# Half of the modulation columns as row sums on VectorE in a two-layer diffusion trunk

## The chip, the cores and the metric

The kernel runs on one core of a Trainium2 chip. The metric is the device time of one execution in microseconds (us); smaller is better. In the profile's names PE is TensorE (matmuls), PEld its weight loads, which overlap the matmuls, DVE is VectorE, ACT ScalarE, POOL GpSimd and SP SyncE, which issues most DMAs. L12 is line 12 of the kernel's source.

## What is computed

Two layers, each with the same weights for 256 latent tokens and 128 context tokens, 1024 wide. The conditioning vectors are `c` for the latent and `c_ctx` for the context tokens.

```
def _modulation(cvec, w_mod, b_mod):
    m = jax.nn.silu(cvec) @ w_mod + b_mod          # 1024 -> 6 x 1024
    return jnp.split(m[:, None, :], 6, axis=-1)

# each layer, for latent and context tokens with their own mod
h = _rms(x, g_mix) * (1.0 + mod[1]) + mod[0]
...                                                # input projection, three groups of attention heads (16 heads)
x = x + mod[2] * (concat(heads) @ w_out)
h = _rms(x, g_ffn) * (1.0 + mod[4]) + mod[3]
ffn = (silu(h @ w_gate) * (h @ w_up)) @ w_down     # 1024 -> 2816 -> 1024
x = x + mod[5] * ffn
```

So a layer has 6 x 1024 modulation values for each of two vectors. The kernel counts them in columns of 128: 0 to 15 are `mod[0]` and `mod[1]` (needed when a layer begins), 16 to 23 `mod[2]` (the attention's gate), 24 to 39 `mod[3]` and `mod[4]` (before the feed-forward), 40 to 47 `mod[5]` (the feed-forward's gate).

## The kernel before

All of it is float32. A big matmul is done as three: weights and activations are split into a high part of reduced precision and the rest, and `mm3` (L318 to L320) adds high x high, high x rest and rest x high. A block of weights arrives from memory in `raw` (three buffers, on SP's queue); ACT makes its high part `wh` (L251), DVE the rest `wl` (L257). The 384 tokens (256 + 128) lie along the free axis, so a matmul is 128x128 by 128x384. In `hh`/`hl`, `fh`/`fl`, `uh`/`ul` lie the two parts of a layer's normalised input, of the feed-forward's input and of its inner activations. PE's results go to PSUM banks named `z`, `s` and `t`.

A layer has four stages:

- *Attention* (layer 0 from the start to about 227 us, layer 1 about 541 to 731): input projection, 16 heads, and the first three of eight blocks of the output projection. Its order on every engine is written out by the kernel itself: a list planner with costs, priorities and earliest times sorts all pieces of work (`add(engine, cost, function, after=..., prio=..., ready=...)`), and the result is emitted as a manual schedule.
- *The rest of the out projection*, blocks m = 3 to 7. `gated` (L502) adds a gated result to the residual `xT`, `gain_split` makes `fh` and `fl`. From here on the framework's scheduler sets the order.
- *Feed-forward up* (L1521 onwards): 22 steps, each with a gate and an up group of 24 matmuls into one bank; then the tokens are scaled by `rb` (L1540), gated (L1545), and split into `uh` and `ul` (L1546, L1547).
- *Feed-forward down*: 8 groups of 66 matmuls and `gated` (L502). After layer 0's, a layer boundary in which a hand-written order on PE mixes the norm with modulation blocks.

The modulation is done by PE in sets of 16 columns (`ModSet`). A block is 128 rows of w_mod by 2048 columns, a load of 1 MB into `raw`; its four matmuls (L369) hold 32 columns of silu(cond) (`sv`) as weights, each in its own column group of the array, over 512 columns of w_mod; eight blocks make a set. Then ACT takes the sums out (`mev`, L375), PE turns them (L380, `t<-ident,mev`) and DVE adds the bias (L386) and writes `mods` (`mod` in the profile); `mod_aff` (L415) makes `aff` from (1 + scale) x gain. Where the sets run:

- layer 0, columns 0 to 15: at the very start, in four parts with their own weights; these blocks have 128 columns by four column groups (`m<-qu,sv`, `m<-ku,sv`).
- layer 0, columns 16 to 31 and 32 to 47: 16 blocks in layer 0's attention, in the planner's list (`blocks`, with earliest times by `SPREAD`).
- layer 1, columns 0 to 15: 8 blocks in layer 0's attention too (`EXTRA`).
- layer 1, columns 16 to 31: blocks 0 to 5 at the layer boundary (`BUB`), the rest in layer 1's attention. The first four come from `early` tiles, loaded by POOL's queue during layer 0's feed-forward, into the room of `hh`, `hl`, `fh` and `fl`.
- layer 1, columns 32 to 47: 8 blocks in layer 1's attention.

`parameters(l)` fetches a row of gains for a layer, spread over the partitions, into `prow` (L534), and DVE makes rotary tables and a lambda of it (L545, L551, L555, L561). For layer 1 it is called in the code between up and down part of layer 0's feed-forward, but waits for nothing there, and the scheduler put it into the end of layer 0's attention.

Of the kernel before, what the change touches and what calls it, by code (L numbers as in the profile page):

```python
# [39 lines left out]
SPREAD = ((15, 3), (60, 9))  # L40
DOWN = (0, 0, 0, 0, 0, 0, 0, 0)

# [136 lines left out]
@with_exitstack  # L179
def trunk(ctx: ExitStack, tc, xT_d, cv_d, pcol_d, prow_d, cache_d, dfk_d, rope_d, bias_d, ident_d,  # L180
          w_mod, w_mod0, w_in, w_uq, w_ukv, w_out, w_gate, w_up, w_down, yT_d, new_d):
    nc = tc.nc
# [151 lines left out]
    class ModSet:  # L334


        def __init__(self, l, q, pre=(), part=None):
            self.l, self.q, self.pre, self.w = l, q, pre, {}
            self.kb = 0
            if part is None:  # L340
                self.n, self.cols = 512, [2048 * q + 512 * g for g in range(4)]
            else:
                n = self.n = 512 // PARTS
                self.cols = [2 * n * part, 2 * n * part + n, 1024 + 2 * n * part, 1024 + 2 * n * part + n]
            self.part, self.step = part, 512 // self.n

        def load(self, kb, *kind):
            if self.part is not None and kind[0] != "raw":
                t = [v.rearrange("p h t -> p (h t)")[:, :1024] for v in self.room()]
            elif self.part is not None:  # L350
                t = raw.tile([P, 2, 1024], F32, tag="raw", name=nm("raw"))
                t = [t[:, i] for i in range(2)]
            if self.part is not None:
                for i in range(2):
                    nc.sync.dma_start(t[i], w_mod0[self.part, kb // self.step, :, i])
                self.w[kb] = [v.rearrange("p (k c) -> p k c", k=self.step) for v in t]
            elif kb < len(self.pre):
                self.w[kb] = self.pre[kb]
            elif self.part is None:
                self.w[kb] = load(mod_rows(self.l, kb, self.cols[0]), [2048])  # L360

        def mm(self, kb):
            if kb == 0:
                self.pm = bank(ps_m, "m")
            w, n = self.w.pop(kb), self.n
            for k in range(self.step):
                for g in range(4):
                    ws = w[:, g * n:(g + 1) * n] if self.part is None else w[g // 2][:, k, (g % 2) * n:(g % 2) * n + n]
                    nc.tensor.matmul(self.pm[32 * g:32 * g + 32, :n], sv[:, kb + k, :], ws,  # L369
                                     start=(kb + k == 0), stop=(kb + k == KD - 1), tile_position=(0, 32 * g))  # L370
            self.kb = kb + self.step
# [10 lines left out]
        def bias(self):  # L382
            nb = self.n // P
            for g in range(4):
                c0 = self.cols[g] // P
                nc.vector.tensor_tensor(  # L386
                    mods[self.l][:, c0:c0 + nb, :], self.pt[:, :nb, 32 * g:32 * g + 2],
                    pcol[self.l][:, PC_BMOD + c0:PC_BMOD + c0 + nb].unsqueeze(2).to_broadcast([P, nb, 2]), op=ALU.add)
            if self.part is not None:
                mod_aff(self.l, 0, KD // PARTS * self.part, KD // PARTS * (self.part + 1))  # L390
            elif self.q != 1:
                mod_aff(self.l, self.q // 2, 0, KD)

        def steps(self):
            for kb in range(self.kb, KD):
                self.load(kb)
                self.mm(kb)
                yield
# [130 lines left out]

    def parameters(l):  # L530

        pc = pcol[l]
        prow = par.tile([P, PR_W], F32, tag="prow", name=nm("prow"))
        fetch = lambda: (nc.sync if l == 0 else nc.gpsimd).dma_start(prow, prow_d[l:l + 1, :].to_broadcast([P, PR_W]))  # L534

# [36 lines left out]
    for l in range(DEPTH):  # L572
        pc = pcol[l]
        prow, naq, nlam, subg, tabs, fetch, stages = made_params
        if l == 0:
            hh = act.tile([P, KD, NT], F32R, tag="hh", name=nm("hh"))
            hl = act.tile([P, KD, NT], F32R, tag="hl", name=nm("hl"))
            early = []
            mod_sets = {key: ModSet(*key, pre=early if key == (1, 1) else ()) for key in ((0, 1), (0, 2), (1, 0), (1, 1), (1, 2))}

# [78 lines left out]
        if l == 0:  # L659
# [776 lines left out]

        blocks = [(ms, kb, SPREAD[l][0] + SPREAD[l][1] * kb) for ms in (mod_sets[l, 1], mod_sets[l, 2]) for kb in range(ms.kb, KD)]
        blocks = [(ms, kb, SPREAD[l][0] + SPREAD[l][1] * i) for i, (ms, kb, _) in enumerate(blocks)]
        if l + 1 < DEPTH:
            blocks += [(mod_sets[l + 1, 0], kb, EXTRA[1] + EXTRA[2] * kb) for kb in range(EXTRA[0])]  # L1440
        prev, fin = None, first_mod
        gates = None
        for i, (ms, kb, r) in enumerate(blocks):
# [44 lines left out]
        if l + 1 < DEPTH:  # L1488
            mod_q.extend(mod_sets[l + 1, q].steps() for q in range(2) if mod_sets[l + 1, q].kb < KD)
        for key, w in ahead:  # L1490
# [26 lines left out]
        ul = ff.tile([P, KF, NT], F32R, name=f"ul{l}")  # L1517
        waiting = []
        for m in range(KF):
            pos = []  # L1520
# [13 lines left out]
            for mm, pos in waiting:  # L1534
# [12 lines left out]
                nc.vector.tensor_tensor(ul[:, mm, :], u, uh[:, mm, :].bitcast(F32), op=ALU.subtract)  # L1547
            waiting = []
        if l + 1 < DEPTH:
            for i in range(4):  # L1550
                pool, tag = (act, "hh") if i == 0 else (act, "hl") if i == 1 else (ff, f"fh{l}") if i == 2 else (ff, f"fl{l}")
                early.append(pool.tile([P, 2048], F32, tag=tag, name=nm("early")))
# [139 lines left out]
```

## Time and profile before

| | us |
|---|---|
| median of three runs | 1043.28 (1042.18 to 1043.92) |
| the profiled execution | 1044.4 |
| its span (first to last instruction) | 1042.2 |
| around the span | 2.2 |
| TensorE busy | 1025.5 (98%) |
| VectorE busy | 630.9 (61%) |
| ScalarE busy | 509.0 (49%) |
| GpSimd busy | 149.9 (14%) |

Starts in the profile count from the span's start. Matmuls are pipelined, and a busy PE need not be at its peak; weight loads (PEld) show how densely matmuls follow each other. PEclk is the granted clock of TensorE as a share of full speed. A view of time windows gives for each window the busy time of PE, PEld, DVE, ACT and POOL with the number of instructions, then the granted clock, the DMA engines' busy share, and GB/s.

### The profile page before, as it was taken

To read this page: it belongs to the slowest core of one execution; us is meant where nothing else is said; L and a number is where in the kernel's file an instruction comes from. 1 tells how busy PE (TensorE), PEld (TensorE's weight loads), DVE (VectorE), ACT (ScalarE), POOL (GpSimd) and SP (SyncE) were. 2 spreads that over 40 slices of the span, in tenths; PEclk is the share of its full clock that TensorE was granted. 3 is DMA by queue.
4 is the path that set the end of the run, shared out by engine and by line. 5 is a ranking of instruction groups with operands and counts; after the bars stand their busy time and mean duration, and the time that the engine had idled before them with its cause. 6 is when DMAs were issued, how large, how long until landed. Compare 5 with 4: busy or idle time off the path is not lost.

```text
span 1042.2 us, 16578 instructions
## 1 busy us (share of the span) xinstructions
PE 1025.5 (98%) x6212; PEld 931.2 (89%) x6212; DVE 630.9 (61%) x1447; ACT 509.0 (49%) x1179; POOL 149.9 (14%) x221
## 2 busy tenths in 40 slices
PE   8999999999999999999999999999999999999998
PEld 7877777669999999999978977777999999999998
DVE  4677786767555555544446887777756555554332
ACT  3376777745433443333326567786644333343221
POOL 2266223200000000000016543240000000000000
PEclk9999999999999999999999999999999999999999
DMA  9865548745625343364444245552334344333541
GB/s 360 317 206 185 165 152 298 256 136 161 203 82 161 93 151 111 96 207 123 128 159 155 73 150 169 189 185 81 122 109 135 110 133 122 120 111 111 148 133 45
DMA packets 125999, 160.14 MB, mean 154 GB/s; under 512 B 4704, under 2 KB 111328, under 8 KB 120800
## 3 DMA queue, kind: packets, MB, share of 16 engines
q1 hardware_dynamic: 123552, 153.73, 45.9%
q0 software_dynamic: 784, 4.69, 1.2%
q8 instruction: 49, 0.80, 0.3%
q10 hardware_dynamic: 1584, 0.66, 0.2%
q14 instruction: 30, 0.25, 0.1%
HBM read 156.02 MB, written 3.05 MB: 153 GB/s over the span
## 4 chain that ended last, share of the span: by engine, by line
PE 88%; POOL 4%; DVE 4%; ACT 2%; issue 1%; DMA 1%; ACTq 0%; DVEq 0%; POOLq 0%
PE z L318 13%; PE z L320 12%; PE z L319 12%; PE t L319 6%; PE t L318 6%; PE t L320 6%; PE s L319 6%; PE s L318 6%; PE s L320 6%; PE m L369 4%; PE s L996 3%; POOL small L510 3%; PE t L963 2%; PE t L1098 2%; PE t L1335 1%
## 5 line engine op out<-in xcount | busy, mean ns | idle before, releaser
L251 ACT ACTIVATE wh<-raw 128x1024 fp32r<-128x1024 f32 (+2 forms) x216 | 201.6, 935 | 356.0 <-PE z L319 128.9
L257 DVE TENSOR_TENSOR wl<-raw,wh 128x1024 fp32r<-128x1024 f32 (+2 forms) x216 | 231.2, 1072 | 122.8 <-ACT wh L251 122.6
L318 PE MATMUL z<-fh,wh 128*128 128x386 f32 x304 | 103.2, 339 | 0.0
L319 PE MATMUL z<-fl,wh 128*128 128x386 f32 x304 | 103.0, 339 | 0.0
L320 PE MATMUL z<-fh,wl 128*128 128x386 f32 x304 | 102.6, 338 | 0.0
L318 PE MATMUL z<-wh,hh 128*128 128x384 f32 (+1 forms) x264 | 100.5, 381 | 0.9 <-ACT tok L1203 0.4
L320 PE MATMUL z<-wh,hl 128*128 128x384 f32 (+1 forms) x264 | 90.4, 342 | 0.5 <-DVE hl L490 0.3
L319 PE MATMUL z<-wl,hh 128*128 128x384 f32 (+1 forms) x264 | 89.7, 340 | 0.0
L510 POOL TENSOR_TENSOR small<-small,mhalf 128x4 f32<-128x4 f32 (+4 forms) x58 | 72.2, 1245 | 4.8
L318 PE MATMUL s<-fh,wh 128*128 128x386 f32 x200 | 68.2, 341 | 0.0
L318 PE MATMUL t<-fh,wh 128*128 128x386 f32 x200 | 68.1, 340 | 0.0
L319 PE MATMUL s<-fl,wh 128*128 128x386 f32 x200 | 67.8, 339 | 0.0
L319 PE MATMUL t<-fl,wh 128*128 128x386 f32 x200 | 67.7, 339 | 0.0
L320 PE MATMUL t<-fh,wl 128*128 128x386 f32 x200 | 67.5, 338 | 0.0
L320 PE MATMUL s<-fh,wl 128*128 128x386 f32 x200 | 67.5, 338 | 0.0
L1015 ACT ACTIVATE e<-s,small 128x384 f32<-128x384 f32 (+1 forms) x108 | 54.3, 509 | 16.3 <-DVE small L1004 15.2
L318 PEld LDWEIGHTS z<-wh,hh 128*128 128x128 f32 x264 | 49.8, 189 | 13.1 <-issue 8.2
L319 PEld LDWEIGHTS z<-fl,wh 128*128 128x128 f32 x304 | 57.5, 189 | 0.0
L320 PEld LDWEIGHTS z<-fh,wl 128*128 128x128 f32 x304 | 57.3, 188 | 0.0
L318 PEld LDWEIGHTS z<-fh,wh 128*128 128x128 f32 x304 | 57.2, 188 | 0.0
L996 PE MATMUL s<-ku,qu 96*128 96x384 f32 (+5 forms) x170 | 52.0, 411 | 0.6 <-ACT e L1015 0.6
L319 PE MATMUL z<-ul,wh 128*128 128x384 f32 x154 | 52.4, 340 | 0.0
(305 smaller groups left out, 2321.1 us busy)
## 6 DMA issues: line engine op xcount, KB each, us to landing
raw<-in_w_mod SPq DMA_DIRECT2D x36, 1024.0 KB, 5.1
raw<-in_w_gate SPq DMA_DIRECT2D x22, 1024.0 KB, 5.4
raw<-in_w_up SPq DMA_DIRECT2D x22, 1024.0 KB, 5.4
raw<-in_w_down SPq DMA_DIRECT2D x32, 704.0 KB, 4.5
raw<-in_w_in SPq DMA_DIRECT2D x40, 384.0 KB, 4.0
raw<-in_w_out SPq DMA_DIRECT2D x8, 1024.0 KB, 5.9
qu<-in_w_mod SPq DMA_DIRECT2D x8, 512.0 KB, 6.7
ku<-in_w_mod SPq DMA_DIRECT2D x8, 512.0 KB, 7.4
```

The source lines that it names most:

```text
L251: nc.scalar.activation(hi, src, AF.Copy)
L257: nc.vector.tensor_tensor(lo, src, hi.bitcast(F32), op=ALU.subtract)
L318: nc.tensor.matmul(out, sh, mh, start=first, stop=False)
L319: nc.tensor.matmul(out, sh, ml, start=False, stop=False)
L320: nc.tensor.matmul(out, sl, mh, start=False, stop=last)
L369: nc.tensor.matmul(self.pm[32 * g:32 * g + 32, :n], sv[:, kb + k, :], ws, start=(kb + k == 0), stop=(kb + k == KD - 1), tile_position=(0, ...
L510: nc.gpsimd.tensor_tensor(out, t[:, :n], mhalf[:, :n], op=ALU.pow)
L963: nc.tensor.transpose(pt[:, b, :], x, ident)
L996: nc.tensor.matmul(ps[:, i, :], q, k, start=True, stop=True)
L1015: nc.scalar.activation(x["e"][i], ps[:, j, :], AF.Exp, bias=x["mx"][:, i:i + 1], accum_out=x["su"][:, i:i + 1])
L1098: nc.tensor.matmul(po[64 * i:64 * i + 64, 0:NL], vv[:, b, v0 + i, :], p["pT"][i][:, b, :], start=(b == 0), stop=(b == 2), tile_position=(0 ...
L1335: nc.tensor.matmul(po, x["p"][:, b, :], vd[0][:, b if t < 2 else 3, h, :], start=(b == 0), stop=(b == nb - 1))
```

## The change

24 columns of the 48 of each layer, but in other places than before, are no longer computed by PE: a column is now 128 row sums of a product, one per partition. Its weights come transposed (`w_modT`, 128x1024, 512 KB) on POOL's queue into a ring of three slots in the room of `hl`; silu of the two vectors, broadcast over the partitions (`crow`, 1 MB), lies in the room of `hh`. For each column and each vector DVE runs one `tensor_tensor_reduce` over 128x1024, which starts from the bias and writes one column of `mods`; it is issued as two instructions, the main one and one that writes out the accumulator (both shown as `ISA` at L444). By layer:

- layer 0: PE keeps columns 16 to 31 (a set of 512-wide blocks, 8) and does 32 to 39 in 4 blocks of two row blocks and 256 columns; 40 to 47 are row sums in layer 0's feed-forward.
- layer 1: PE keeps 16 to 31; 0 to 15 and 32 to 39 are row sums in layer 0's feed-forward, 40 to 47 in layer 1's.

In layer 0's feed-forward that makes 32 columns (64 row sums), in layer 1's 8 (16). `ROWS_UP` and `ROWS_DOWN` say after which step of the loops the code issues how many columns; the scheduler places them. The loads of the `early` tiles move behind the last row sum. The parameter row of layer 1 lands in a tile in the room of `fl` (`staged`), which is free only after the last up matmul, and ACT copies it to `prow`.

```diff
@@ numbers
-DOWN = (0, 0, 0, 0, 0, 0, 0, 0)
+ROWSUMS = ((0, (40, 48)), (1, (0, 16)), (1, (32, 40))), ((1, (40, 48)),)
+ROWS_UP = (0, 0) + (1,) * 20
+ROWS_DOWN = (2, 3, 3, 4, 0, 0, 0, 0)
-EXTRA = (8, 135, 7)
@@ new class
+    class RowSums:
+        def __init__(self, parts):
+            self.todo = [(l, c) for l, (a, b) in parts for c in range(a, b)]
+            room = act.tile([P, 3 * DM], F32, tag="hh", name=nm("sums"))
+            self.s, self.junk = room[:, :2 * DM].rearrange("p (v k) -> p v k", v=2), room[:, 2 * DM:]
+            self.w = act.tile([P, 3, DM], F32, tag="hl", name=nm("wt"))
+            self.n = self.loaded = 0
+            nc.gpsimd.dma_start(self.s, crow_d.unsqueeze(0).to_broadcast([P, 2, DM]))
+            self.load()
+            nc.scalar.activation(self.s, self.s, AF.Silu)
+        def load(self):
+            while self.loaded < min(self.n + 3, len(self.todo)):
+                l, c = self.todo[self.loaded]
+                nc.gpsimd.dma_start(self.w[:, self.loaded % 3], w_modT[l, c * P:(c + 1) * P])
+                self.loaded += 1
+        def step(self, n):
+            for l, c in self.todo[self.n:self.n + n]:
+                for v in range(2):
+                    nc.vector.tensor_tensor_reduce(self.junk, self.w[:, self.n % 3], self.s[:, v], 1.0,
+                                                   pcol[l][:, PC_BMOD + c:PC_BMOD + c + 1], ALU.mult, ALU.add, mods[l][:, c, v:v + 1])
+                self.n += 1
+                self.load()
+                if l and c in (15, 39):
+                    mod_aff(l, c // 32, 0, KD)
@@ parameters
-        fetch = lambda: (nc.sync if l == 0 else nc.gpsimd).dma_start(prow, prow_d[l:l + 1, :].to_broadcast([P, PR_W]))
+        def fetch():
+            rows = prow_d[l:l + 1, :].to_broadcast([P, PR_W])
+            if staged is None:
+                nc.sync.dma_start(prow, rows)
+            else:
+                t = staged.tile([P, PR_W], F32, tag=f"fl{l - 1}", name=nm("staged"))
+                nc.gpsimd.dma_start(t, rows)
+                nc.scalar.activation(prow, t, AF.Copy)
@@ trunk: the sets
-            mod_sets = {key: ModSet(*key, pre=early if key == (1, 1) else ()) for key in ((0, 1), (0, 2), (1, 0), (1, 1), (1, 2))}
+            mod_sets = [[ModSet(0, 512, [2 * DM]), ModSet(0, 256, [4 * DM])], [ModSet(1, 512, [2 * DM], pre=early)]]
...
-        if l + 1 < DEPTH:
-            blocks += [(mod_sets[l + 1, 0], kb, EXTRA[1] + EXTRA[2] * kb) for kb in range(EXTRA[0])]
+        blocks = [(ms, kb) for ms in mod_sets[l] for kb in range(ms.kb, KD, ms.step)]
+        blocks = [(ms, kb, SPREAD[l][0] + SPREAD[l][1] * i) for i, (ms, kb) in enumerate(blocks)]
@@ feed-forward
+        sums = RowSums(ROWSUMS[l])
...
+            sums.step(ROWS_UP[m])
         if l + 1 < DEPTH:
-            for i in range(4):
-                ...
-                nc.gpsimd.dma_start(early[i], mod_rows(l + 1, i, 2048))
-            made_params = parameters(l + 1)
+            made_params = parameters(l + 1, ff)
...
-                if m < 7:
-                    mod_steps(DOWN[m])
+                sums.step(ROWS_DOWN[m])
+                if sums.n == len(sums.todo) and not early:
+                    for i, (pool, tag) in enumerate(((ff, f"fh{l}"), (ff, f"fl{l}"), (act, "hh"), (act, "hl"))):
+                        early.append(pool.tile([P, 2048], F32, tag=tag, name=nm("early")))
+                        nc.gpsimd.dma_start(early[i], mod_rows(l + 1, i, 2048))
```

`ModSet` now takes its columns as runs of a given width; a block of n columns by four groups covers 512 / n blocks of rows.

The first place is DVE in an up step of layer 0's feed-forward. `wl` is the rest of a weight block, `gt` the scaled and gated results, `ul` the rest of the inner activations. Before:

```order
L1538 COPY small_3796<-s_3740 128x2
L1540 TENSOR_TENSOR gt_3798<-s_3740,rb_3345 128x384
L257 TENSOR_TENSOR wl_3769<-raw_3765,wh_3767 128x1024
L1538 COPY small_3800<-t_3771 128x2
L1540 TENSOR_TENSOR gt_3802<-t_3771,rb_3345 128x384
L1545 SCALAR_TENSOR_TENSOR gt_3802<-gt_3802,small_3800,gt_3798 128x256
L1545 SCALAR_TENSOR_TENSOR gt_3802<-gt_3802,small_3800,gt_3798 128x128
L257 TENSOR_TENSOR wl_3812<-raw_3734,wh_3810 128x1024
L1547 TENSOR_TENSOR ul_3347<-gt_3802,uh_3346 128x384
```

And after (`sums` is the room with silu of the vectors, `wt` the ring of weights):

```order
L1578 COPY small_4278<-s_4224 128x2
L1580 TENSOR_TENSOR gt_4280<-s_4224,rb_3274 128x384
L444 ISA sums_3277,mod_102<-wt_3278,sums_3277,pcol_106 128x1024
L444 ISA mod_102 128x1
L260 TENSOR_TENSOR wl_4251<-raw_4172,wh_4249 128x1024
L1587 TENSOR_TENSOR ul_3276<-gt_4209,uh_3275 128x384
L444 ISA sums_3277,mod_102<-wt_3278,sums_3277,pcol_106 128x1024
L444 ISA mod_102 128x1
L1578 COPY small_4282<-t_4253 128x2
L1580 TENSOR_TENSOR gt_4284<-t_4253,rb_3274 128x384
L260 TENSOR_TENSOR wl_4299<-raw_4295,wh_4297 128x1024
```

Row sums stand ahead of each `wl`, two or three to a step. The second place is DVE at the end of layer 0's attention, from the last head's output `o` to the first `wl` that the out projection waits for. Before:

```order
L386 TENSOR_TENSOR mod_102<-t_3023,pcol_106 128x8 x4
L415 SCALAR_TENSOR_TENSOR aff_104<-mod_102,pcol_106 128x16
L1113 TENSOR_TENSOR o_2838<-t_3059,o_2837 128x384
L1512 TENSOR_TENSOR fl_3129<-mod_101,fh_3128 128x8x2
L502 SCALAR_TENSOR_TENSOR xT<-z_2825,mod_101,xT 128x256
L502 SCALAR_TENSOR_TENSOR xT<-z_2825,mod_101,xT 128x128
L502 SCALAR_TENSOR_TENSOR xT<-z_3003,mod_101,xT 128x256
L502 SCALAR_TENSOR_TENSOR xT<-z_3003,mod_101,xT 128x128
L257 TENSOR_TENSOR wl_3106<-raw_2681,wh_3089 128x1024
```

After:

```order
L1154 TENSOR_TENSOR o_2589<-t_3001,o_2588 128x384
L1551 TENSOR_TENSOR fl_3058<-mod_101,fh_3057 128x8x2
L534 SCALAR_TENSOR_TENSOR xT<-z_2741,mod_101,xT 128x256
L534 SCALAR_TENSOR_TENSOR xT<-z_2741,mod_101,xT 128x128
L534 SCALAR_TENSOR_TENSOR xT<-z_2791,mod_101,xT 128x256
L534 SCALAR_TENSOR_TENSOR xT<-z_2791,mod_101,xT 128x128
L534 SCALAR_TENSOR_TENSOR xT<-z_2986,mod_101,xT 128x256
L534 SCALAR_TENSOR_TENSOR xT<-z_2986,mod_101,xT 128x128
L529 SCALAR_TENSOR_TENSOR fl_3058<-xT,aff_103,fh_3057 128x256
L529 SCALAR_TENSOR_TENSOR fl_3058<-xT,aff_103,fh_3057 128x128
L529 SCALAR_TENSOR_TENSOR fl_3058<-xT,aff_103,fh_3057 128x256
L464 TENSOR_TENSOR sq_3039<-sq_3039,sq_3043 128x384
```

Directly behind it stands the `wl` of the out projection's block m = 3: three gates and four rows of the norm are now ahead of it, where two gates were. On PE the same place reads as follows after the change (`oxh` and `oxl` are the two parts of the head outputs that are ready early, `z_3071` is block m = 3):

```order
L321 MATMUL z_2986<-o_2588,wh_2637 128x384
L322 MATMUL z_2986<-o_2589,wh_2637 128x384
L323 MATMUL z_2986<-o_2588,wl_2839 128x384
L321 MATMUL z_3071<-oxh_133,wh_3030 128x384
L322 MATMUL z_3071<-oxl_134,wh_3030 128x384
L321 MATMUL s_3115<-oxh_133,wh_3074 128x384
L322 MATMUL s_3115<-oxl_134,wh_3074 128x384
L321 MATMUL z_3155<-oxh_133,wh_3078 128x384
L322 MATMUL z_3155<-oxl_134,wh_3078 128x384
L323 MATMUL z_3071<-oxh_133,wl_3048 128x384
```

Six matmuls that use only `wh` are ahead of the first that uses `wl_3048`. The third place is DVE where the down part begins; `prow`, `tab` and `lp` are layer 1's parameters, which stood in layer 0's attention before, and `raw_5066` is the weight block of the second down group:

```order
L586 TENSOR_SCALAR prow_4988<-prow_4988 128x32
L592 TENSOR_TENSOR tab_4993<-rope,prow_4988 128x2x32
L596 TENSOR_TENSOR tab_4993<-rope,prow_4988 128x2x2x8 x2
...
L602 TENSOR_TENSOR lp_5016<-prow_4988 128x64
L444 ISA sums_3277,mod_102<-wt_3278,sums_3277,pcol_106 128x1024
L444 ISA mod_102 128x1
L592 TENSOR_TENSOR tab_4995<-rope,prow_4988 128x2x32
L596 TENSOR_TENSOR tab_4995<-rope,prow_4988 128x2x2x8 x2
L260 TENSOR_TENSOR wl_5070<-raw_5066,wh_5068 128x768
```

The tables wait for the parameter rows, and the `wl` of the down part stands behind them.

More of the change, by code (lines that the diff above doesn't have):

```diff
@@ L334, in trunk @@
     class ModSet:
-        def __init__(self, l, q, pre=(), part=None):
-            self.l, self.q, self.pre, self.w = l, q, pre, {}
-            self.kb = 0
-            if part is None:
-                self.n, self.cols = 512, [2048 * q + 512 * g for g in range(4)]
-            else:
[L343 to L360, printed above, removed]
@@ new lines, in __init__, with load @@
+        def __init__(self, l, n, runs, part=None, pre=()):
+            self.l, self.n, self.part, self.pre, self.w = l, n, part, pre, {}
+            self.runs, self.per = runs, 4 // len(runs)
+            self.cols = [c + n * i for c in runs for i in range(self.per)]
+            self.step = 512 // n
+            self.kb = 0
+        def load(self, kb, *kind):
+            if kb < len(self.pre):
+                self.w[kb] = [self.pre[kb].rearrange("p (k c) -> p k c", k=1)]
+                return
+            nr, width = len(self.runs), self.n * self.per
+            if kind and kind[0] == "un":
+                t = [v.rearrange("p h t -> p (h t)")[:, :1024].rearrange("p (k c) -> p k c", k=self.step) for v in self.room()]
+            else:
+                t = raw.tile([P, nr, self.step, width], F32, tag="raw", name=nm("raw"))
+                t = [t[:, i] for i in range(nr)]
+            for i, c in enumerate(self.runs):
+                src = w_mod[self.l, kb * P:(kb + self.step) * P, c:c + width].rearrange("(k p) c -> p k c", p=P)
+                if self.part is not None:
+                    src = w_mod0[self.part, kb // self.step, :, i].rearrange("p (k c) -> p k c", k=self.step)
+                nc.sync.dma_start(t[i], src)
+            self.w[kb] = t
@@ L367, in mm @@
                 for g in range(4):
-                    ws = w[:, g * n:(g + 1) * n] if self.part is None else w[g // 2][:, k, (g % 2) * n:(g % 2) * n + n]
-                    nc.tensor.matmul(self.pm[32 * g:32 * g + 32, :n], sv[:, kb + k, :], ws,
+                    i = g % self.per
+                    nc.tensor.matmul(self.pm[32 * g:32 * g + 32, :n], sv[:, kb + k, :], w[g // self.per][:, k, i * n:(i + 1) * n],
                                      start=(kb + k == 0), stop=(kb + k == KD - 1), tile_position=(0, 32 * g))
@@ L390, in bias @@
                 mod_aff(self.l, 0, KD // PARTS * self.part, KD // PARTS * (self.part + 1))
-            elif self.q != 1:
-                mod_aff(self.l, self.q // 2, 0, KD)
+            elif self.cols[0] == 4 * DM:
+                mod_aff(self.l, 1, 0, KD)
         def steps(self):
-            for kb in range(self.kb, KD):
+            for kb in range(self.kb, KD, self.step):
                 self.load(kb)
@@ L1488, in trunk @@
         if l + 1 < DEPTH:
-            mod_q.extend(mod_sets[l + 1, q].steps() for q in range(2) if mod_sets[l + 1, q].kb < KD)
+            mod_q.extend(ms.steps() for ms in mod_sets[l + 1])
         for key, w in ahead:
@@ L1670 @@
     arrays, args = {}, []
-    order = ("xT", "cv", "pcol", "prow", "cache", "dfk", "rope", "bias", "ident", "w_mod", "w_mod0", "w_in", "w_uq", "w_ukv", "w_out", "w_gate", "w_up", "w_down")
+    order = ("xT", "cv", "crow", "pcol", "prow", "cache", "dfk", "rope", "bias", "ident", "w_mod", "w_mod0", "w_modT", "w_in", "w_uq", "w_ukv", "w_out", "w_gate", "w_up", "w_down")
     for n, v in ((n, feeds[n]) for n in order):
```

18 lines of the change are left out of this document (8 added, 10 removed).

## The prediction, made before the changed kernel was run

> **What bounds the kernel now.** I read the page first: the busy shares, the strips and the shares of the chain that ended last.
>
> ```profile
> span 1042.2 us, 16578 instructions
> PE 1025.5 (98%) x6212; PEld 931.2 (89%) x6212; DVE 630.9 (61%) x1447; ACT 509.0 (49%) x1179; POOL 149.9 (14%) x221
> ...
> PE   8999999999999999999999999999999999999998
> PEld 7877777669999999999978977777999999999998
> ...
> PEclk9999999999999999999999999999999999999999
> ...
> PE 88%; POOL 4%; DVE 4%; ACT 2%; issue 1%; DMA 1%; ACTq 0%; DVEq 0%; POOLq 0%
> ```
>
> TensorE works 98% of the span and carries 88% of the chain, so work taken from it should shorten the run. But the weight loads (PEld) fall to 6 to 8 tenths in two stretches, the two attention stages, and are full elsewhere. The next view gives each engine's busy time in stretches: layer 0's attention (four rows), the out projection's end, a feed-forward, and layer 1's attention (three rows).
>
> ```profile
> 100.00:150.00 50.00, 49.09 (x306) 35.88 (x305) 40.11 (x108) 36.93 (x124) 15.62 (x27) 1.00 0.56 182
> 150.00:200.00 50.00, 50.00 (x352) 36.10 (x350) 33.90 (x92) 34.25 (x113) 9.99 (x20) 1.00 0.78 268
> 200.00:225.00 25.00, 22.88 (x133) 14.75 (x130) 20.56 (x73) 15.83 (x46) 5.98 (x9) 0.93 0.54 173
> 225.00:265.00 40.00, 40.00 (x239) 39.11 (x237) 25.13 (x50) 20.46 (x38) 1.11 (x2) 1.00 0.48 163
> 300.00:350.00 50.00, 50.00 (x285) 50.00 (x284) 28.96 (x54) 20.03 (x30) 0.00 (x0) 1.00 0.40 125
> 600.00:650.00 50.00, 47.26 (x294) 36.70 (x295) 39.67 (x105) 35.98 (x115) 18.91 (x25) 1.00 0.49 161
> 650.00:700.00 50.00, 50.00 (x327) 39.36 (x327) 38.03 (x97) 39.62 (x130) 17.96 (x32) 1.00 0.57 189
> 700.00:730.00 30.00, 28.66 (x181) 20.48 (x175) 22.39 (x70) 19.30 (x62) 2.82 (x5) 0.94 0.26 86
> ```
>
> The first three numbers of a row after the length are PE, PEld and DVE. In the feed-forward (300 to 350) loads run 50.00 of 50: a saturated TensorE. From 150 to 200 PE also reads 50.00, but PEld 36.10, that is 0.72. There part of PE's "busy" is head work that a dependence stretches, and the dense matmuls and modulation blocks fill holes between the heads. DVE is at 0.68 to 0.80 there and at 0.58 in the feed-forward.
>
> The Trainium skill (Perfetto Trace Analysis, Identifying the Most-Contended Engine) says that matmul busy time is no good measure of how full TensorE is and that the busy share of weight loads is. By busy time the removed work would be worth all of itself, by the loads about seven tenths; the rows above agree with the page so far as the two do part in attention and not in the feed-forward.
>
> **1. Modulation blocks leave TensorE.** A block is four matmuls of 512 columns (8 records). Its tile's rows, two blocks in the chain, and a set's turn:
>
> ```profile
> L369 PE MATMUL m<-raw,sv x288: 592/593/1062, 52.6 to 707.3; 128*32 128x512 f32 x144
> L369 PE MATMUL m<-early,sv x32: 592/592/617, 537.4 to 542.6; 128*32 128x512 f32 x32
> ...
> 189.29 1.00 PE m L369 x8
> ...
> 220.36 1.87 PE m L369 x8
> ...
> 223.97 0.60 PE L380 MATMUL t<-ident,mev 128*128 128x128 f32 x4
> ```
>
> That is 320 records, 40 blocks, at 1.00 us each (the row at 189.29; the one at 220.36 ran at a low clock). In layer 0's attention stood 24 of them: the two sets of columns 16 to 47, and layer 1's first set. Now 8 blocks of 512 columns and 4 of two rows of 256 columns, as long by their elements, stand there: 12 fewer, 12.0 us. Layer 1 has 8 where it had 16: 8.0 us. A set also ends in a turn of 0.60: one and a half fewer in layer 0 (a half set has half a turn), one in layer 1. In all 12.9 + 8.6 = 21.5 us. The evacuations on ACT and the bias sums on DVE behind them go too; both engines have slack there, so they count nothing.
>
> What of it reaches the end lies between 0 (the heads' chains bind and holes merely stay empty) and 1. By the loads, 0.72 to 0.79 of TensorE's time in the main windows is real feed, and 0.59 (14.75 of 25) in layer 0's tail, 200 to 225, where heads run without enough filler. After the change that tail has 105 rows behind the last input-projection matmul on PE in place of 62 (135 for 107 in layer 1), so I take 0.65, between the two: **-14.0 us**; ends 0 and -21.5.
>
> **2. Layer 1's parameter rows leave layer 0's attention tail.** These stood there:
>
> ```profile
> 209.18 0.65 POOL L534 DMA_DIRECT2D prow<-in_prow  x1 [0.30 <-POOL brief L1162]
> 209.18 5.93 DMA prow<-in_prow
> 215.21 0.18 DVE L545 TENSOR_SCALAR prow<-prow 128x32 f32<-128x32 f32 x1 [1.03 <-DMA prow<-in_prow]
> 217.88 0.52 PE L963 MATMUL t<-ident,e 128*128 128x128 f32 x3 [2.11 <-DVE small L1020]
> ```
>
> DVE waited 1.03 us for the landing and then put the tables in front of a head's softmax; TensorE stood still 2.11 us, and the granted clock of that window was 0.93, 1.75 us of 25. Now nothing of it is there. At most 2.11 + 1.75 = 3.9 us come back; at least nothing, if the head is late anyway. I take **-3.0**: the wait goes surely, part of the clock's dip may stay in a tail with less filler.
>
> **3. The handover to layer 0's out projection.** In the new DVE order three pairs of gates, three modulated rows and a sum of squares stand before the first weight remainder (wl); before it was two pairs of gates. The rows that price them, and, for the next part, those of the feed-forward (300 to 400):
>
> ```profile
> L502 DVE SCALAR_TENSOR_TENSOR xT<-z,mod,xT 128x256 f32<-128x256 f32 x3 | 1.5, 484 | 3.6 <-PE z L320 3.6
> L502 DVE SCALAR_TENSOR_TENSOR xT<-z,mod,xT 128x128 f32<-128x128 f32 x3 | 1.0, 342 | 0.0
> ...
> L257 DVE TENSOR_TENSOR wl<-raw,wh 128x1024 fp32r<-128x1024 f32 x24 | 29.3, 1222 | 4.1 <-ACT wh L251 4.1
> L1547 DVE TENSOR_TENSOR ul<-gt,uh 128x384 fp32r<-128x384 f32 x12 | 6.6, 551 | 0.0
> L1545 DVE SCALAR_TENSOR_TENSOR gt<-gt,small,gt 128x256 f32<-128x256 f32 x12 | 5.8, 484 | 1.3
> L1540 DVE TENSOR_TENSOR gt<-z,rb 128x384 f32<-128x384 f32 x10 | 5.5, 549 | 0.0
> L1545 DVE SCALAR_TENSOR_TENSOR gt<-gt,small,gt 128x128 f32<-128x128 f32 x12 | 4.1, 346 | 0.0
> ...
> 197.99 1.22 DVE L257 TENSOR_TENSOR wl<-raw,wh 128x1024 fp32r<-128x1024 f32 x1
> 199.12 0.41 DVE L1179 TENSOR_REDUCE small<-brief 128x4 f32<-128x256 f32 x1
> ...
> 255.85 0.34 PE L318 MATMUL z<-fh,wh 128*128 128x386 f32 x1
> 443.73 0.34 PE L319 MATMUL s<-fl,wh 128*128 128x386 f32 x1
> 443.91 0.34 PE L320 MATMUL s<-fh,wl 128*128 128x386 f32 x1
> 444.08 0.34 PE L318 MATMUL z<-uh,wh 128*128 128x384 f32 x1
> ```
>
> On a full DVE the next instruction starts 0.09 us before the last one's end (197.99 to 199.12 is 1.13, not 1.22). So a pair costs 0.40 + 0.25, three pairs 1.95, the rows at the same shapes 1.05, the squares 0.46 (as 0.551 for 128x384), the remainder 1.13: 4.6 us from the first finished sum. TensorE has 12 matmuls to do meanwhile (the last six use wh alone), at 0.18 each (443.73 to 443.91) 2.1 us, and then waits: **+2.5**, between 0 (the sums finish earlier than I think) and 4.6. Before, 225 to 265 shows no idle time.
>
> **4. Row sums on VectorE.** No row of before has this instruction. Each column has two, each over 128x1024 with two fp32 inputs, and each is followed by an accumulator read. The nearest rows are L257, the same size with two inputs, and ACT's accumulator read:
>
> ```profile
> 198.69 0.21 ACT L1015 ACTIVATION_READ_ACCUMULATOR e<-s,small 128x1 f32 x1
> 198.78 0.59 ACT L1015 ACTIVATE e<-s,small 128x384 f32<-128x384 f32 x1
> ```
>
> Low end 1.13 + 0.09 = 1.22 us, high end 1.22 + 0.21 = 1.43; I take 1.3, as the reads follow closely. The order puts 59 of the 64 row sums of layer 0's feed-forward between the second up step and the second down step, some 21.5 up steps of 8.56 us ((444.08 - 255.85) / 22; the up part's first matmul is at 255.85): 184 us. DVE is free for 21.04 of 50 us there, so 77 us, 1.31 a row sum; taking the 0.09 off each of some nine instructions a step (two remainders, one rest of the product, six for the gating) frees 17 us more and makes it 1.6. 59 x 1.3 = 77 us fits, but nearly fills an in-order queue in which the wl of TensorE's next group stands behind one or two row sums. I count **+1.0**; ends 0 and (1.43 - 1.31) x 59 = +7. In layer 1's feed-forward 16 take 21 us of as much room: nothing.
>
> The Trainium skill (Vector Engine (DVE) Microarchitecture Reference, Points that are easy to get wrong) warns that the scalar-tensor-tensor shape with two sources in SBUF that are not bf16 runs at half rate, for want of a port for the accumulator. Against it stand the L1545 rows, which have such sources: 484 - 346 = 138 ns for 128 more elements, 1.08 ns each, as L257 has; but they don't use the accumulator, so the trace doesn't decide. At half rate a row sum would cost about 2.36; what that makes is the second rival.
>
> The weights of the sums (32 x 512 KB in 184 us, 91 GB/s beside 125, DMA share 0.40) come on POOL's queue, which has three slots, each due two columns (about 11 us) later, against 5.93 us for the landing above. ACT's one Silu of 128x2048 falls where ACT is free for 30 of 50 us. Both: nothing. The early loads of layer 1's blocks now start in the down part, behind the last sums, and have 50 us or more until 537: nothing.
>
> **5. The rows land after the last up matmul.** The landing slot is free at 444.08. With 5.93 us, an ACT copy behind one or two splits, and some dozen DVE instructions of 0.2 us, DVE reaches the next remainder about 10.4 to 11.8 us later; TensorE asks for it after one down group, 66 matmuls of 0.176, 11.6 us. **+0.5**, ends 0 and +3 if the landing is slow.
>
> **Sum.** -14.0 - 3.0 + 2.5 + 1.0 + 0.5 = -13.0. The profiled execution took 1044.4 us (span 1042.2 and 2.2 around it): 1031.4. It stands 1.1 above the median of 1043.28, so 1030.3: I say 1030.
>
> **Rivals.** *Everything taken off counts*, and the handover is hidden: -21.5 - 3.9 and nothing against it, 1018. For it: PE 50.00 of 50. Against: PEld 36.10.
> *Row sums too dear.* If one costs 2.36 us, 59 of them lack (2.36 - 1.45) x 59 = 54 us of room (1.45 is the middle of 1.31 and 1.6); DVE then sets the pace of layer 0's up part: 1084, slower. It decides from 1.45 + 13/59 = 1.67 us on; at 1.5 to 1.67 the run is between 1033 and 1043. The extrapolated slope of two-input rows speaks against it.
> *Heads bind.* The blocks filled holes that stay empty: only the rows' wait comes back, less the three losses: -3.0 + 4.0 = +1, about 1044; with a third of the credit (-7) 1037. For it: the tail's 0.59 and DVE's 40.11 of 50. Against: the tail without enough filler is 25 us long, the stretch in which blocks were spread over 100.
>
> **Chances.** Forecast (1020 to 1037) 0.57; full credit 0.12; heads bind 0.17, most of it between 1037 and 1043, some within a two-thousandth of before; row sums too dear 0.14, a fifth of that still faster. 0.2% is 2.1 us, about what a measurement of this kernel can tell from no change. Faster 0.83, same 0.05, slower 0.12. The range, 1016 to 1042, leaves out the dear row sums and the ends.
>
> **What would show it.** Right: L444's main row about 1.15 to 1.25 us, its read about 0.1 to 0.2; 300 to 350 with PE and PEld 50 of 50 and DVE above 0.9; layer 0's attention 8 us shorter or so, layer 1's 5; no prow row before the down part; one PE wait of 2 to 3 us at layer 0's out projection, released by a DVE wl. Wrong: PEld below 0.97 in layer 0's up part with PE waiting for wl (row sums), or the first out-projection matmul of a layer at the old time with lower PE share in the attention (heads).

## The result, and the profile after

The changed kernel takes 1036.14 us (median of four, 1035.75 to 1036.68) against 1042.73 us for the kernel before on the same chip (1041.92 to 1043.92): a ratio of 0.9935, 95% interval 0.9920 to 0.9949, so 6.6 us or 0.65% faster. The prediction said 1030, range 1016 to 1042. The time is in the range and the direction is right, but the gain is half of the 13 us forecast. The experiments show that the blocks moved out of layer 0's attention brought about what was forecast and that those moved out of layer 1's cost time. With two further losses, some 2 us are left of it beside the 4.2 us that the parameter rows bring alone.

The page of the changed kernel: span, busy shares, the strips of 40 slices, and the chain.

```profile
span 1034.4 us, 16528 instructions
PE 1012.3 (98%) x6074; PEld 933.0 (90%) x6074; DVE 719.5 (70%) x1599; ACT 509.1 (49%) x1180; POOL 172.7 (17%) x263
...
PE   8999999989999999999999999989999999999998
PEld 7877779679999999999978878867999999999998
...
PEclk9999999989999999999999999969999999999999
...
PE 76%; DVE 2%; ACT 1%; POOL 1%; issue 1%; ACTq 0%; DVEq 0%; POOLq 0%
L444 DVE CUSTOM_DVE_ANT_0 sums<-wt,sums,pcol 128x1024 f32<-128x1024 f32 x80 | 102.2, 1278 | 0.3 <-DVE small L1578 0.3
```

DVE has 89 us more work, as planned, and PE 13 us less. The 80 row sums are 40 columns of the 96 of both layers, 8 of layer 0 and 32 of layer 1, not 24 of each layer. The line to look at is PEclk: before it was 9 in every slice, now there is an 8 and a 6. Over the whole span the granted clock fell:

```profile
core 0: 1042.2 us, clock 0.995
```

```profile
core 0: 1034.4 us, clock 0.986
```

The first row is before, the second after. Before lost 0.005 x 1042.2 = 5 us of TensorE's clock, after 14.5 us, although after does less on TensorE. Where this happens shows in windows of the changed kernel (columns: PE, PEld, DVE, ACT, POOL busy, granted clock, DMA share, GB/s). First the end of layer 0's attention, then layer 1's attention tail, then layer 0's up part, and the start of the down part:

```profile
220.90:227.73 6.83, 4.41 (x14) 4.41 (x15) 5.98 (x10) 2.04 (x6) 0.00 (x0) 0.50 0.47 147
674.88:678.29 3.41, 2.29 (x15) 1.68 (x14) 2.53 (x7) 2.99 (x12) 2.95 (x5) 1.00 0.77 261
678.29:698.77 20.48, 18.98 (x61) 11.92 (x63) 13.61 (x41) 12.15 (x43) 5.82 (x11) 0.50 0.05 14
698.77:702.18 3.41, 3.41 (x27) 2.98 (x24) 2.55 (x7) 2.44 (x7) 0.44 (x1) 1.00 0.21 58
245.00:433.00 188.00, 188.00 (x1071) 187.73 (x1070) 170.88 (x316) 75.37 (x115) 17.99 (x33) 1.00 0.64 210
433.00:480.00 47.00, 47.00 (x270) 45.92 (x269) 28.63 (x61) 16.64 (x23) 3.18 (x6) 1.00 0.75 234
```

From 678.29 to 698.77 TensorE ran at exactly half clock, for six times 3.41 us, and PE reads 18.98 of 20.48. The chain that ended last stays on PE from 678.62 to 699.66 but for some 1.2 us, so PE is the bound there, at half speed. The layer's last input-projection matmul starts at 673.99; what follows is heads alone, where before the modulation blocks stood between them. The window ahead of the drop has PE busy for 2.29 of 3.41 us only.

The stages, each from its first matmul to the next stage's, in us; the last column is (1 - granted clock) x span, to about 0.5 us, since the clock has three digits.

| | layer 0: attention and out projection | up | down and boundary | layer 1: attention and out projection | clock lost |
|---|---|---|---|---|---|
| before | 233.5 | 188.2 | 100.9 | 212.5 | 5.2 |
| after | 224.4 | 188.3 | 102.2 | 213.5 | 14.5 |
| rows only (e3) | 229.6 | 188.3 | 100.9 | 210.9 | 1.0 |
| rows early (e4) | 230.1 | 188.3 | 102.3 | 213.6 | 17.7 |
| earlier wl (e2) | 220.3 | 188.3 | 102.2 | 213.5 | 10.3 |
| spare matmuls (e1) | 224.7 | 188.2 | 102.2 | 209.2 | 3.1 |
| L1 blocks back (e5) | 225.0 | 188.2 | 100.9 | 211.1 | 3.1 |

Layer 0's attention gained 9.1 us, layer 1's, with 8 blocks fewer, lost 1.0, and the down part lost 1.3. Of what the prediction named as signs of being right, layer 0's attention shorter by some 8 us has come and layer 1's by 5 has not. Against the kernel with the parameter rows alone (e3), which has no half clock in either attention, layer 1's attention lost 2.6 us.

### The profile page after: what moved, and what is told of

It is laid out like the page before. It is cut to its first block, busy times and chain, and to the rows that moved or that the text cites. A ratio compares the mean times of both kernels' runs of the same rounds, so it can differ in the third digit from the quotient of the medians.

```text
span 1034.4 us, 16528 instructions
## 1 busy us (share of the span) xinstructions
PE 1012.3 (98%) x6074; PEld 933.0 (90%) x6074; DVE 719.5 (70%) x1599; ACT 509.1 (49%) x1180; POOL 172.7 (17%) x263
## 4 chain that ended last, share of the span: by engine, by line
PE 76%; DVE 2%; ACT 1%; POOL 1%; issue 1%; ACTq 0%; DVEq 0%; POOLq 0%
PE z L321 11%; PE z L323 11%; PE z L322 11%; PE t L322 6%; PE t L321 6%; PE t L323 6%; PE s L322 5%; PE s L323 5%; PE s L321 5%; PE s L1037 2%; PE t L1004 2%; PE t L1139 1%; POOL small L542 1%; PE t L1376 1%; PE z L1037 1%
## 5 line engine op out<-in xcount | busy, mean ns | idle before, releaser
L444 DVE CUSTOM_DVE_ANT_0 sums<-wt,sums,pcol 128x1024 f32<-128x1024 f32 x80 | 102.2, 1278 | 0.3 <-DVE small L1578 0.3
L438 POOL DMA_DIRECT2D wt<-in_w_modT x40 | 21.5, 539 | 273.7 <-DVE mod L444 190.8
L1056 ACT ACTIVATE e<-s,small 128x384 f32<-128x384 f32 (+1 forms) x102 | 51.0, 506 | 12.2 <-DVE small L1045 11.2
```

The source lines that it names most:

```text
L438: nc.gpsimd.dma_start(self.w[:, self.loaded % 3], w_modT[l, c * P:(c + 1) * P])
L444: nc.vector.tensor_tensor_reduce(self.junk, self.w[:, self.n % 3], self.s[:, v], 1.0, pcol[l][:, PC_BMOD + c:PC_BMOD + c + 1], ALU.mult, A ...
L1056: nc.scalar.activation(x["e"][i], ps[:, j, :], AF.Exp, bias=x["mx"][:, i:i + 1], accum_out=x["su"][:, i:i + 1])
```

## The experiments

All times are medians of runs beside the kernel before on the same chip (1042.1, 1042.4 and 1041.8 us in the three groups), three rounds each unless said. The changed kernel itself was not run in these groups, so that differences to it are between groups, whose medians of the kernel before differ by up to 0.9 us.

**e3: of the change only the parameter rows.**

```diff
+            made_params = parameters(l + 1, ff)
+            made_params[-2]()
+            for _, _, f in made_params[-1]:
+                f()
             for i in range(4):
...
-            made_params = parameters(l + 1)
-            made_params[-2]()
-            for _, _, f in made_params[-1]:
-                f()
```

This is the kernel before with the change's `fetch` in `parameters`, called ahead of the early loads.

> The kernel before, with one thing of the change: layer 1's parameter rows land in fl's room after the up part and are copied by ACT, and the early loads follow them. No row sums, all modulation blocks on TensorE. By the prediction's step: -3.0 for the stall in layer 0's attention tail, +0.5 to +1.4 for the wait where the down part begins: 1040 to 1041. Rival (the head was late anyway): 1042.7 or up to 1.4 more.

Measured 1037.92 us, ratio 0.9962 (0.9947 to 0.9977): 4.2 us faster, more than the forecast for this step. The stop in layer 0's tail is gone, and with it the half-clock window behind it; the same stretch before and in this run:

```profile
200.00:225.00 25.00, 22.88 (x133) 14.75 (x130) 20.56 (x73) 15.83 (x46) 5.98 (x9) 0.93 0.54 173
...
200.00:225.00 25.00, 25.00 (x162) 17.96 (x160) 18.67 (x57) 15.89 (x46) 4.17 (x7) 1.00 0.54 180
```

The down part stays at 100.9 us: the rows' late landing costs nothing there.

**e4: the change without that step.**

```diff
-                nc.sync.dma_start(prow, rows)
+                (nc.sync if l == 0 else nc.gpsimd).dma_start(prow, rows)
...
-            made_params = parameters(l + 1, ff)
+            made_params = parameters(l + 1)
```

> The changed kernel, with layer 1's parameter rows fetched straight to their place as before (no landing tile, no ACT copy), which lets them move back into layer 0's attention tail. By the prediction's step the stall returns and the wait at the down part goes: +1.5 to +2.5, 1037.5 to 1038.5. Rival (without the modulation blocks the tail has room on DVE): the stall costs nothing and the 1.4 us at the down part's start come back: 1034.5 to 1036.

Measured 1042.70 us, ratio 1.0004 (0.9992 to 1.0015). Both expectations were too low. With all 20 blocks moved to VectorE and the rows where they were, the kernel is no faster than before at all. Its granted clock is the lowest of these runs but for e6:

```profile
core 0: 1040.1 us, clock 0.983
```

So of the change's 6.6 us, 4.2 come from the parameter rows alone, and the rest of the change adds 1.8 where the rows are out of the way (1037.9 to 1036.1) and nothing where they aren't. The modulation's 20 us of TensorE work were thus nearly worthless, or something took them back. The next runs show the second.

**e1: work added where the clock drops.**

```diff
+HOLD = (20, 115, 0.8)
...
+            def hold(k):
+                if not spare:
+                    spare["pm"] = bank(ps_m, "m")
+                for _ in range(k):
+                    nc.tensor.matmul(spare["pm"][:, :P], ones, ones, start=True, stop=True)
+            for i in range(HOLD[0]):
+                prev = add(PE, 0.43, lambda: hold(2), after=[prev, fin], prio=DENSE + 9, ready=HOLD[1] + HOLD[2] * i)
```

> The changed kernel with 40 spare 128x128 matmuls of a tile of ones (20 pairs, written to the modulation's free bank and read by nobody) in the places of layer 1's attention tail where the planner has nothing for TensorE. The changed kernel's trace shows the granted clock at 0.50 from about 678 to 698 us, right after the last input-projection matmul (673.99). Theory (the clock): the tail has gaps since its modulation blocks are gone, the clock is halved for some 20 us, and PE was busy for most of them; with the gaps filled the clock stays at 1.00 and the run falls by 5 to 8 us, to 1028 to 1031, although work was added. Rival (the heads' chain through ACT and DVE sets the tail): the clock comes back but the time stays within 2 us of 1036.1, or rises by up to the 8 us that the spare matmuls cost.

Measured 1032.16 us, ratio 0.9904 (0.9889 to 0.9918): 4.0 us faster than the changed kernel, with 80 useless matmul records added, some 8.6 us of TensorE (20 of them take from 695.73 to 697.88):

```profile
695.73 2.39 PE L1505 MATMUL m<-ones 128*128 128x128 f32 x20
697.88 0.42 PE L1038 MATMUL s<-ku,qu 128*128 128x128 f32 x2
```

Layer 1's tail in the changed kernel, and in this run:

```profile
660.00:700.00 40.00, 37.38 (x183) 29.17 (x182) 27.32 (x71) 26.28 (x86) 10.40 (x18) 0.74 0.32 101
...
660.00:700.00 40.00, 40.00 (x283) 36.00 (x283) 32.49 (x85) 31.03 (x101) 10.35 (x18) 1.00 0.33 103
```

The granted clock is 1.00 in place of 0.74, and PE does 283 records (spare ones included) in place of 183. The rival, that the heads' chain through ACT and DVE sets the tail, falls: layer 1's attention got shorter by 4.3 us (213.5 to 209.2) with all of that work still there. The planner orders some of the heads' pieces differently around the spare matmuls (the `t<-identr,tok` at 686.47 of the changed kernel stand behind the next `vd,pd` here), and no run separates what that order is worth from the clock. The gain is a little under the 5 to 8 that was expected.

**e5: layer 1's blocks back on TensorE.** The same test with real work.

```diff
-ROWSUMS = ((0, (40, 48)), (1, (0, 16)), (1, (32, 40))), ((1, (40, 48)),)
+ROWSUMS = ((0, (40, 48)), (1, (0, 16))), ()
-ROWS_DOWN = (2, 3, 3, 4, 0, 0, 0, 0)
+ROWS_DOWN = (2, 2, 0, 0, 0, 0, 0, 0)
...
-            mod_sets = [[...], [ModSet(1, 512, [2 * DM], pre=early)]]
+            mod_sets = [[...], [ModSet(1, 512, [2 * DM], pre=early), ModSet(1, 512, [4 * DM])]]
```

> The changed kernel with layer 1's columns 32 to 47 back on TensorE: 8 blocks of 512 columns in layer 1's attention, as before the change, and no row sums for them (24 columns are left in layer 0's feed-forward, none in layer 1's). Theory (the clock): the blocks are 8.6 us of TensorE work, but they keep the clock up in the tail, so that the stretch from the first input-projection matmul to the first feed-forward matmul of layer 1 is no longer than the changed kernel's 213.5 us (211 to 213), and the run is 1033.5 to 1036. Rival (the prediction's step 1, by which these blocks' work counts at 0.65): 5.6 us slower than the changed kernel, 1041 to 1042.

Measured 1032.78 us, ratio 0.9911 (0.9895 to 0.9928): 3.4 us faster than the change, with 8.6 us more on TensorE, slightly better than the clock theory's range and far from the 1041 to 1042 of the prediction's pricing. Layer 1's tail has its clock:

```profile
660.00:700.00 40.00, 39.47 (x261) 30.57 (x261) 31.59 (x85) 33.79 (x109) 13.02 (x22) 1.00 0.56 187
```

Of the 3.4 us, 2.4 are in layer 1's attention (213.5 to 211.1). Another 1.3 are in the down part (102.2 to 100.9), where with fewer row sums the early tiles are loaded sooner; e11 is about that loss. In layer 1's attention the blocks' cost was thus below nothing: they held the clock up for the heads.

**e2: the handover of layer 0.** The changed kernel's trace shows what came between the attention and the out projection (PE, ACT and DVE rows):

```profile
216.67 2.01 ACT L254 ACTIVATE wh<-raw 128x1024 fp32r<-128x1024 f32 x2 [2.05 <-PE z L322]
216.85 2.04 DVE L534 SCALAR_TENSOR_TENSOR xT<-z,mod,xT 128x256 f32<-128x256 f32 x6 [1.66 <-PE z L323]
...
218.73 0.45 PE L321 MATMUL s<-oxh,wh 128*128 128x384 f32 x1 [0.32 <-ACT wh L254]
...
220.08 0.45 PE L321 MATMUL z<-oxh,wh 128*128 128x384 f32 x1 [0.72 <-ACT wh L254]
...
221.57 0.56 DVE L464 TENSOR_TENSOR sq<-sq,sq 128x384 f32<-128x384 f32 x1
222.05 3.49 DVE L260 TENSOR_TENSOR wl<-raw,wh 128x1024 fp32r<-128x1024 f32 x3
...
223.32 0.69 PE L323 MATMUL z<-oxh,wl 128*128 128x384 f32 x1 [2.62 <-DVE wl L260]
```

The wait that the prediction named is there, released by the wl that it named. The edit lets the planner place the two splits of that weight block before the third gate:

```diff
-            hi, lo, w, lead = weights(("out", l, m, 0), lead if m % 2 else None, prio=DENSE + 1)
+            hi, lo, w, lead = weights(("out", l, m, 0), lead if m % 2 else None, prio=DENSE + 1 if l else DENSE - 1)
```

> The changed kernel with the weight splits of out-projection block m = 3 of layer 0 given a higher priority in the planner, so that DVE makes the wl that TensorE waits for after two gates in place of three gates, three modulated rows and a sum of squares. In the changed kernel's trace TensorE idles 0.32 + 0.72 + 2.62 us there and runs 4.3 us at half clock behind it (about 2 us lost). Theory (the wait at the handover): 3 to 5 us come back, 1031 to 1033. Rival (the delayed gates and rows become the next wait): 1035 to 1037.

Measured 1032.34 us, ratio 0.9906 (0.9889 to 0.9922): 3.8 us faster than the change, within the theory's range. The two stretches, changed kernel and this run:

```profile
200.00:240.00 40.00, 36.26 (x202) 31.23 (x201) 26.29 (x64) 21.42 (x52) 0.00 (x0) 0.91 0.25 78
...
200.00:240.00 40.00, 38.82 (x229) 34.67 (x230) 28.52 (x66) 22.43 (x50) 0.00 (x0) 1.00 0.34 106
```

2.6 us of PE time and all of the clock came back; layer 1 is as in the change (213.5 us).

**e7 and e9: both edits, and with fewer spare matmuls.**

> Both edits together on the changed kernel: the 40 spare matmuls in layer 1's attention tail (1032.2 alone) and the earlier wl at layer 0's handover (1032.3 alone). If the two losses are separate, they add: 1036.1 - 4.0 - 3.8 = 1028.3, within 1.0. If one loss only moves into the other's place: 1031 to 1032.5.

> As the run with both edits, with only the first 18 of the 40 spare matmuls, those within the first microseconds behind layer 1's last input-projection matmul. If those gaps are what halves the clock, it stays up with less added work: 1026.5 to 1028.3. If the clock needs work over the whole tail, it drops later in the tail and the run is 1029 to 1032.5.

e7 takes 1028.69 us, ratio 0.9869 (0.9855 to 0.9884): the two losses are separate and add (1028.3 was expected). e9 takes 1029.11 us (0.9862 to 0.9897 as a ratio). The times of the two overlap, but the trace decides: the last spare matmul of e9 is at 681.6 us, and its clock held for some 15 us more and then dropped later in the tail, as the second expectation had it:

```profile
682.00:689.00 7.00, 7.00 (x44) 4.99 (x45) 6.42 (x22) 5.64 (x21) 1.11 (x2) 1.00 0.10 28
689.00:696.00 7.00, 6.45 (x42) 4.82 (x38) 6.58 (x19) 5.34 (x18) 0.00 (x0) 1.00 0.12 30
696.00:707.00 11.00, 10.64 (x41) 6.85 (x42) 8.21 (x26) 5.97 (x20) 1.11 (x2) 0.53 0.00 1
```

So the place right behind the dense matmuls isn't the only one at which the clock can fall: the tail needs work further on too.

**e10: layer 1's blocks back and the earlier wl**, the version without useless work.

> Layer 1's 8 blocks back on TensorE (1032.8 alone) and the earlier wl at layer 0's handover (1032.3 alone), no spare matmuls. If the two gains are separate, as the clock theory has it: 1032.8 - 3.8 = 1029.0, within 1.0, with the clock lost for less than 4 us in all. If the 8 blocks' own work counts once the clock is held: 1031 or more, over 2 us behind the run with spare matmuls (1028.7).

Measured 1028.32 us, ratio 0.9865 (0.9851 to 0.9880), within the first expectation: 13.5 us faster than before, 7.8 faster than the change.

**e11: the early tiles in another order of rooms**, on e7's kernel.

```diff
-                    for i, (pool, tag) in enumerate(((ff, f"fh{l}"), (ff, f"fl{l}"), (act, "hh"), (act, "hl"))):
+                    for i, (pool, tag) in enumerate(((act, "hh"), (act, "hl"), (ff, f"fh{l}"), (ff, f"fl{l}"))):
```

> The run with spare matmuls and earlier wl (1028.7), with the four early tiles in another order of rooms (hh, hl, fh, fl in place of fh, fl, hh, hl). In the changed kernel the first early block lies in fh, is loaded soon after the up part, and the scheduler puts its matmuls into the middle of the second down group (at 445.70), where TensorE has no gap. With the other order it stands at the layer boundary again. If that block is what makes the changed kernel's down part 1.4 us longer (93.9 in place of 92.5 us): 1.0 to 1.4 us faster, 1027.3 to 1027.7. If it only moves into the boundary's own chain: 1028.7 within 0.5. If the parameter rows' late landing is the cause, as the prediction's step 5 would have it, the down part stays at 93.9.

Measured 1027.38 us, ratio 0.9861 (0.9844 to 0.9877), 1.3 us under e7 in the median. The runs of the two overlap (1026.41 to 1028.69 here, 1028.08 to 1029.81 there), so the time alone settles little; but the down part's matmuls take 92.5 us in place of 93.9. In the changed kernel an early block stood in the middle of a down group:

```profile
445.70 1.06 PE L372 MATMUL m<-early,sv 128*32 128x512 f32 x8
...
446.69 0.44 PE L323 MATMUL s<-uh,wl 128*128 128x384 f32 x1
```

Every run with the first early block inside a down group (the change, e1, e2, e4, e6, e7, e9) has 93.9 to 94.1 us there, and every run with it at the boundary (before, e3, e5, e10, e11) has 92.5. That block, which the early tile's new room let the scheduler pull out of the layer boundary, is the change's loss in the down part.

**e6: the row sums twice** (a single run).

```diff
-                for v in range(2):
+                for v in (0, 1) * (2 if DOUBLE and len(self.todo) > 8 else 1):
```

> The changed kernel with each row sum of layer 0's feed-forward made twice in a row (the second writes the same value). A row sum takes 1.28 + 0.08 us in the trace; DVE is busy 47.4 of 50 us there. If DVE then sets the pace as in the prediction's rival, about 118 in the up part need 160 us of some 87 us of room: 60 to 80 us slower, 1096 to 1116. If the room is larger than reckoned (DVE's busy time shrinks when it is packed), less than 40 us slower.

Measured 1082.0 us, 45.9 above the changed kernel; neither range holds it. The up part still takes 188.2 us. The scheduler kept 57 row sums there, as many as in the changed kernel, and put the rest behind. The bill came at the layer boundary, where TensorE waited for early blocks whose loads are issued only behind the last sum:

```profile
500.00:550.00 50.00, 31.90 (x188) 30.90 (x186) 47.23 (x80) 10.62 (x14) 4.67 (x8) 0.83 0.60 202
```

```profile
569.47 1.28 DVE L445 CUSTOM_DVE_ANT_0 sums<-wt,sums,pcol 128x1024 f32<-128x1024 f32 x1
...
571.06 1.06 POOL L1613 DMA_DIRECT2D early<-in_w_mod  x2 [15.42 <-DVE aff L419]
...
576.28 1.93 PE L373 MATMUL m<-early,sv 128*32 128x512 f32 x8 [43.30 <-DMA early<-in_w_mod]
```

The down part and the boundary took 147.9 us (435.27 to 583.12) against 102.2, which is the whole difference.

## Why the prediction was right, and where it was not

*Step 1, the modulation blocks (-14.0): about right for layer 0, wrong in sign for layer 1.* With 0.65 of the 12.9 and 8.6 us that it priced, the step stands for 8.4 us in layer 0 and 5.6 in layer 1. With the rows out of the way in both and the handover mended, layer 0's attention went from 229.6 us (e3) to 220.3 (e2): 9.3 us. Layer 1's went from 210.9 (e3) to 213.5 (after): 2.6 us lost, so that step 1 as a whole gave 6.7. What failed is the share of 0.65 in layer 1: it asked how much of TensorE's time in the attention was real feed, and took for granted that the clock of what is left stays as it was. The prediction saw a granted clock of 0.93 in layer 0's tail and the longer tails in the order, but drew no line from one to the other. Layer 1's tail then ran 20.48 us at half clock; with the clock held, 8.6 us of spare work made layer 1's attention 4.3 us shorter (e1), and 8.6 us of real work 2.4 (e5).

*Step 2, the parameter rows (-3.0, ends 0 and -3.9).* Mechanism right: -4.2 alone (e3), with an interval (-5.5 to -2.4) that holds the forecast. Within the change it is -6.6 (e4 to after); e4 pays more clock (17.7 us lost, 14.5 after), and that the thinner tail has less to cover a stop with is not shown.

*Step 3, the handover (+2.5).* Place, releaser and mechanism right. The idle time is 0.32 + 0.72 + 2.62 = 3.7 us, since ACT's norm rows and wh splits stood in the chain too, which the sum left out. The clock stands at half from 220.90 to 227.73, from within the wait to behind it, with PE busy for 4.41 of these 6.83 us. Mending it was worth 3.8 us (e2).

*Step 4, the row sums (+1.0).* The main instruction takes 1.28 us and its successor starts 1.21 after it:

```profile
331.38 1.28 DVE L444 CUSTOM_DVE_ANT_0 sums<-wt,sums,pcol 128x1024 f32<-128x1024 f32 x1
332.59 0.08 DVE L444 DVE_READ_ACCUMULATOR2_ANT mod<- 128x1 f32 x1
332.59 0.15 DVE L1578 COPY small<-z 128x2 f32<-128x2 f32 x1
```

That is the low end of the bounds (1.22), and the up part took 188.3 us as before: the cost is nil. The half rate that the Trainium skill's page (Vector Engine (DVE) Microarchitecture Reference, Points that are easy to get wrong) gives the scalar-tensor-tensor shape does not show here: by the prediction's estimate from it a row sum would take about 2.36 us, and 1.28 was measured. No run shows whether this instruction counts as that shape. The rival's break-even (1.67 us) was reckoned for the up part alone; e6 shows that the scheduler moves what is too much out of the up part, and that it is paid at the boundary.

*Step 5, the rows' landing at the down part (+0.5).* No wait: the rows came in time, and e3's down part is unchanged. The 1.3 us that the down part did lose are the moved early block, a term that the sum didn't have.

Added up from these runs: -9.3 and +2.6 for the blocks, -4.2 for the rows, +4.1 for the handover (224.4 to 220.3 in layer 0), nothing for the sums, +1.3 for the early block, in all -5.5, where -6.6 was measured with an interval from -8.3 to -5.3. So the time fell into the range by its width: the forecast was 8.2 us too good for layer 1's blocks, 1.6 for the handover, and lacked the 1.3 of the early block, and small errors the other way made up for a part. For step 1 in layer 1 that is luck. The range's slow end stood for the rival in which heads bind. That rival's result was near (1037 to 1043), but not its mechanism: holes did not stay empty at the same pace; TensorE slowed down in them.

## What to carry to other kernels

Filler work on TensorE between latency-bound chains can also hold its clock; before taking it away, look at the granted clock where filler is thin already, and price the tail at half speed. Take filler from stretches that stay dense without it and leave it where the chain is sparse: here the version that keeps layer 1's last 8 blocks (e5, 1032.8 us) beats the one that moves them (1036.1). With the earlier wl it takes 1028.3 (e10), and moving all of them does as well if spare matmuls take their place (e7, 1028.7, and e11, 1027.4). When one change holds several edits, run each alone: here one of them, the parameter rows, brings 4.2 of the 6.6 us by itself, and a gain of 9.3 and several losses hide in the rest.

## What the runs showed of the hardware

A few sparse microseconds can be followed by twenty at half clock. In layer 1's tail a window with PE busy 2.29 of 3.41 us was followed by 20.48 us at half clock, in which PE was busy for 18.98. Before, the sparser window 215.62 to 219.03 was followed by only one at half clock, and the window at 553.51, with PE busy 2.08, by none:

```profile
215.62:219.03 3.41, 1.29 (x12) 0.79 (x10) 3.34 (x20) 1.62 (x5) 0.00 (x0) 1.00 0.49 168
219.03:222.44 3.41, 3.41 (x16) 1.19 (x17) 3.15 (x8) 2.03 (x6) 0.00 (x0) 0.50 0.00 0
222.44:225.85 3.41, 3.41 (x23) 3.35 (x24) 1.21 (x8) 1.64 (x6) 0.00 (x0) 1.00 0.74 245
...
553.51:556.92 3.41, 2.08 (x8) 1.30 (x8) 2.33 (x5) 1.99 (x5) 1.45 (x4) 1.00 0.63 218
556.92:560.34 3.42, 3.42 (x20) 3.39 (x19) 1.75 (x6) 2.00 (x6) 1.55 (x2) 1.00 0.00 2
```

So PE's busy share in a window doesn't say by itself when the clock falls. Nor do weight loads say when it rises: the window at 219.03, behind which it rose, has 1.19 us of them, and the six of the changed kernel 11.92, which is 2 us each. PE reads full in the first and in three of the six. Which measure of activity moves the clock is not settled. The Trainium skill (TensorE: Matmul & The Clock Gate, Part 1) has the gate drop to half after an idle window of some 3.4 us and rise after a busy one; the length of the window and the half rate agree with these rows, an idle window was not needed here, and one that reads busy was not enough.

The kernel before shows the two going together without any edit. Its 13 runs beside e1 to e4 range from 1039.66 us (granted clock 1.000, span 1037.5) to 1045.12 us (0.995, span 1043.0): 5.5 us of span against 0.005 x 1043 = 5.2 us of lost clock. What in these runs starts a drop, and what the stop ahead of it costs by itself, they don't show.
